# Smaller first part and more seven-product pairs in a feed-forward block, on one core

## The chip, the cores and the metric

The kernel runs on one core of a Trainium2 chip. The metric is device time in microseconds (us) for one launch. Engines are named as in the profile: PE is the matrix engine (TensorE; its weight loads stand apart as PEld), DVE is VectorE, ACT is ScalarE, POOL is GpSimd, SP issues the weight loads. L146 is line 146 of the kernel before.

## The reference, cut to what matters

The kernel computes two layers of an encoder for 256 tokens of width 2048, all in float32: attention in the first, a recurrent block in the second, and behind each a feed-forward block. The change touches the feed-forward block:

```python
x = x + swiglu(rms_norm(x, norm_ffn[i]), ffn_w_gate[i], ffn_w_up[i], ffn_w_down[i])

def swiglu(h, w_gate, w_up, w_down):          # w_gate, w_up: 2048 x 5632, w_down: 5632 x 2048
    return (jax.nn.silu(h @ w_gate) * (h @ w_up)) @ w_down
```

## The kernel before, in words

**Products.** A float32 product is made of three matmuls. A weight tile of 128 x 1024 lands in SBUF (`raw`), ACT rounds it to a high part (`hi`, L145 and L163) and DVE subtracts that to give a low part (`lo`, L146 and L164); activations are split the same way. `product` (L321) then issues high x high, low x high and high x low, each with 512 moving columns.

**Units.** The 5632 hidden features are 44 tiles of 128. A unit is 4 of them; there are 11 units, 0 to 10. `unit` (L754) computes gate and up for its four tiles over the 2048-wide contraction, which is cut into 8 pairs (c = 0 to 7) of two tiles. A pair is done in one of two ways. An *ordinary* pair takes two halves (a gate and an up tile), each 12 matmuls, 24 in all. A *seven-product* pair (`load_seven`, L154) treats the 2 x 2 blocks of weights by Strassen's scheme: 7 products, 21 matmuls. It pays with six more DVE instructions of 512 columns and three more ACT casts: with weight blocks b11, b21 and t1, b22 it needs t1 = b11 + t1 (on DVE at L174 if the three loads ahead were ordinary ones, else by an accumulating DMA that POOL issues at L176), t2 = t1 + b22, t3 = t2 - b11, t4 = b21 + t2 (L169), and a high part (L170) and a low part (L171) of t2, t3 and t4. PE takes them in the order b11, b21, t1, b22, t2, t3, t4. `SEVEN` names the pairs done this way, six of eight; `FEWER` gives shorter lists for the first units.

**End of a unit.** DVE adds up the products (L770 to L773, L791, L794; behind ACT's copy at L769), ACT applies SiLU, DVE multiplies (L795) and transposes 32 x 32 blocks (L408), ACT copies them into place (L416, 16 copies), then ACT and DVE make the high and low part of the hidden tile (L801, L802). With `beside` the copies and the last step are put into `tail` and taken out one piece per `load_seven` of the next unit, 4 copies a piece; without it all 16 stand in one lump.

**Parts.** The down projection is cut along the hidden features into parts (`PARTS`, in tiles). When a part's units are done, its four groups of 512 output columns are computed, two behind each of the next units (`ffn_plan`, L208). Each group is a chunk of 12 matmuls per two hidden tiles. Its two results are scaled by ACT out of PSUM (`form`, L818, two buffers) and added to `x` by an accumulating DMA of POOL (L821). ACT results of every second group are held in `parted` and ordered behind the last cast of the following seven-product pair. The last part goes through `groups` (L355) and DVE.

**What sets the order.** PE's order is the order of the code. A scheduler orders the other engines, within rules: `behind` chains all casts among each other and all DVE work of a split (key "rest") among each other; `ahead` keeps some instructions in front of a coming one. Each engine runs its queue in order. SP loads the weights through 8 `raw` buffers, 7 pairs of `hi`/`lo` hold the parts.

Of the kernel before, what the change touches and what calls it, by code (L numbers as in the profile page):

```python
# [12 lines left out]
F32 = mybir.dt.float32  # L13
# [11 lines left out]
GROUP = NQ // NKV  # L25
NBLK = 8
DFF = 5632
PARTS = [8, 8, 8, 8, 12]
UNIT = 4
SEVEN = (0, 1, 2, 4, 5, 6)  # L30
FEWER = {0: (0, 5, 6), 1: (4, 5, 6), 2: (1, 4, 5, 6)}
HALF = 8
CHUNK = HALF * P
WIDE = 512
# [40 lines left out]
def trunk(ctx, tc, w, out):  # L75
# [17 lines left out]
    def tmp(tag, shape=(P, S), dt=F32, bufs=2):  # L93
        pl = tp if tag in COMMON else scope[-1]
        return pl.tile(list(shape), dt, tag=tag, name=nm(tag), bufs=bufs)
# [9 lines left out]
        )  # L105


    ring, held, ft, ahead, tail, parted = [0], [], [], [], [], []

    def parts(shape):  # L110
        n = ring[0] = (ring[0] + 1) % (RING + MORE)
# [42 lines left out]
    def load_seven(srcs, soon):  # L154
# [20 lines left out]
        else:  # L175
            pool.dma_start(out=t1, in_=b11, accum_op=ALU.add)  # L176
        two(raw[0], ("b11", "b21"))
        two(raw[1], ("t1", "b22"))
        if tail:
            tail.pop(0)()  # L180
        one = [tmp(t, (P, WIDE), F32R) for t in ("ohi", "olo")]
        hi, lo = parts([P, 2, WIDE])
        got["t2"] = tuple(one)
        got["t3"], got["t4"] = ((hi[:, j, :], lo[:, j, :]) for j in range(2))
        t2 = b22
        rests = [
            combine(t2, t1, b22, ALU.add, *got["t2"]),
            combine(b11, t2, b11, ALU.subtract, *got["t3"]),
            combine(b21, t2, b21, ALU.add, *got["t4"]),
        ]  # L190
        while parted:
            follow(parted.pop(), newest["cast"])
        for rest in rests:
            rest()
        return got
# [198 lines left out]
    pool.memset(ones, 1.0)
    idle = ps_m.tile([P, P], F32, tag="pm", name=nm("pm"))
# [354 lines left out]
    def ffn(norm, nxt):  # L750
# [60 lines left out]
        ends = np.cumsum(PARTS) // UNIT  # L811
        for what, i in ffn_plan():
            if what == "unit":
                hid[int(np.searchsorted(ends, i, "right"))] += unit(FEWER.get(i, SEVEN), 0 < i < ends[-1] - 1, (act,) if i < ends[-1] - 1 else (act, dve), i < ends[0])
            else:
                for a, acc in enumerate(wide_project(hid[i[0]], PARTS[i[0]], bank)):
                    t = tmp("form", (P, WIDE))
                    m = act.activation(t, acc, AF.Copy, scale=norm.r[:, a : a + 1])  # L818
# [224 lines left out]
```

## Time and profile before

| | |
|---|---|
| median of 3 runs | 1952.31 us (1952.17 to 1952.49) |
| the profiled execution | 1952.89 us, its span 1951.1 us |
| PE, PEld, DVE, ACT, POOL busy | 99%, 83%, 91%, 74%, 21% of the span |
| matmuls | 9224 |
| granted PE clock | 1.00 |
| first layer's feed-forward | starts near 266 us, ends near 950 us |
| second layer's | starts near 1263 us, ends with the kernel |

A row of the timeline reads: start, busy time, engine, line, operation, output<-inputs, shape, count, and in brackets how long the engine was idle ahead of it and what ended that. A busy time includes the part that overlaps the next instruction on the same engine, so the price of an instruction in a row of them is the distance between starts. A row of the windows has the window's length, then busy time and count for PE, PEld, DVE, ACT and POOL; its count takes in instructions that hang over an edge.

### The profile page before, as it was taken

Reading aid. Unit: us, or ns where it says so; the run is one execution under the profiler, and the core shown is the slowest. Engines: PE = TensorE matmul, PEld = TensorE weight load, DVE = VectorE, ACT = ScalarE, POOL = GpSimd, SP = SyncE. Lnnn points to the kernel's source line nnn. Section 1 sums busy time; section 2 is a strip of 40 time slices with the busy share of each in tenths; the row PEclk is TensorE's granted clock in tenths of the full one; section 3 lists DMA queues with packets and bytes.
Section 4 is the critical chain, followed back from the end, with each engine's and each line's share of the span. In section 5 each row is a group of like instructions: output and inputs, shape, how many; then the busy total and the mean of one; then the engine's idle time right before and its main releaser. Section 6 shows DMA issues by size and latency. Waiting matters only on the chain.

```text
span 1951.1 us, 27630 instructions
## 1 busy us (share of the span) xinstructions
PE 1938.0 (99%) x9224; PEld 1624.0 (83%) x9224; DVE 1768.6 (91%) x2417; ACT 1448.3 (74%) x2358; POOL 401.3 (21%) x497
## 2 busy tenths in 40 slices
PE   9999999999999999999999999999999999999999
PEld 8898888788888888888899998887888888888887
DVE  7878698999999999998799997898999999999993
ACT  7677686777777777777698887866778776787772
POOL 0442250011101111010465450520101111011100
PEclk9999999999999999999999999999999999999999
DMA  8434746698878978787365556555878888788872
GB/s 328 156 127 152 248 158 197 196 272 236 248 233 243 262 240 246 235 244 246 126 223 188 189 164 245 175 194 174 253 236 248 245 248 253 231 246 251 246 257 86
DMA packets 131727, 426.42 MB, mean 219 GB/s; under 512 B 14720, under 2 KB 14976, under 8 KB 131584
## 3 DMA queue, kind: packets, MB, share of 16 engines
q1 hardware_dynamic: 108944, 383.21, 58.0%
q0 software_dynamic: 22496, 41.43, 11.9%
q8 instruction: 72, 1.18, 0.2%
q14 instruction: 71, 0.58, 0.1%
q10 hardware_dynamic: 144, 0.02, 0.0%
HBM read 382.13 MB, written 2.10 MB: 197 GB/s over the span
## 4 chain that ended last, share of the span: by engine, by line
PE 92%; DVE 4%; ACT 1%; issue 1%; DMA 1%; POOL 0%; SPq 0%; ACTq 0%; DVEq 0%; POOLq 0%
PE acc L326 14%; PE acc L323 14%; PE acc L324 14%; PE pm L326 11%; PE pm L323 11%; PE pm L324 11%; PE acc L294 8%; PE acc L292 4%; PE pm L306 1%; PE pm L307 1%; PE pm L305 1%; DVE lo L146 1%; ACT hi L145 1%; DVE lo L164 0%; DMA raw<-in_w_in_dram 0%
## 5 line engine op out<-in xcount | busy, mean ns | idle before, releaser
L146 DVE TENSOR_TENSOR lo<-raw,hi 128x1024 fp32r<-128x1024 f32 (+1 forms) x474 | 574.5, 1240 | 77.1 <-ACT hi L145 75.3
L145 ACT CAST hi<-raw 128x1024 fp32r<-128x1024 f32 (+1 forms) x474 | 478.4, 1045 | 116.5 <-PE acc L324 72.1
L326 PE MATMUL acc<-lo,xg 128*128 128x512 f32 x744 | 290.9, 391 | 2.0 <-DVE lo L146 1.8
L323 PE MATMUL acc<-hi,xg 128*128 128x512 f32 x744 | 290.0, 390 | 0.0
L324 PE MATMUL acc<-hi,xg 128*128 128x512 f32 x744 | 289.6, 389 | 0.0
L164 DVE TENSOR_TENSOR lo<-raw,hi 128x1024 fp32r<-128x1024 f32 x232 | 275.0, 1217 | 6.5 <-ACT hi L163 3.8
L294 PE MATMUL acc<-xg,hi 128*128 128x512 f32 x832 | 271.7, 397 | 0.6 <-ACT hi L145 0.6
L163 ACT CAST hi<-raw 128x1024 fp32r<-128x1024 f32 x232 | 234.6, 1048 | 41.0 <-issue 14.4
L176 POOL DMA_DIRECT2D raw<-raw x90 | 77.7, 863 | 903.9 <-DVE raw L174 369.5
L323 PE MATMUL pm<-hi,act 128*128 128x512 f32 x512 | 199.2, 389 | 0.0
L324 PE MATMUL pm<-hi,act 128*128 128x512 f32 x512 | 199.2, 389 | 0.0
L326 PE MATMUL pm<-lo,act 128*128 128x512 f32 x512 | 199.2, 389 | 0.0
L416 ACT COPY two<-one 32x256 f32<-32x256 f32 x420 | 169.7, 404 | 24.7 <-DVE one L408 16.5
L292 PEld LDWEIGHTS acc<-xg,lo 128*128 128x128 f32 x832 | 156.3, 188 | 35.4 <-DVE lo L146 2.8
L323 PE MATMUL acc<-hi,act 128*128 128x512 f32 x448 | 174.9, 390 | 0.4 <-DVE two L794 0.4
L326 PE MATMUL acc<-lo,act 128*128 128x512 f32 x448 | 174.4, 389 | 0.0
L324 PE MATMUL acc<-hi,act 128*128 128x512 f32 x448 | 174.4, 389 | 0.0
L292 PE MATMUL acc<-xg,lo 128*128 128x256 f32 x832 | 171.8, 281 | 1.2 <-DVE lo L146 1.2
L326 PEld LDWEIGHTS acc<-lo,xg 128*128 128x128 f32 x744 | 139.7, 188 | 34.1 <-DVE lo L146 5.4
L324 PEld LDWEIGHTS acc<-hi,xg 128*128 128x128 f32 x744 | 139.7, 188 | 29.2
L323 PEld LDWEIGHTS acc<-hi,xg 128*128 128x128 f32 x744 | 139.7, 188 | 28.6
L170 ACT CAST hi<-raw 128x512 fp32r<-128x512 f32 x232 | 137.1, 622 | 32.8 <-DVE raw L169 31.8
(221 smaller groups left out, 3852.1 us busy)
## 6 DMA issues: line engine op xcount, KB each, us to landing
raw<-in_w_gate_dram SPq DMA_DIRECT2D x176, 512.0 KB, 4.6
raw<-in_w_up_dram SPq DMA_DIRECT2D x176, 512.0 KB, 5.5
raw<-in_w_down_dram SPq DMA_DIRECT2D x176, 512.0 KB, 4.4
raw<-in_w_in_dram SPq DMA_DIRECT2D x64, 512.0 KB, 4.4
raw<-raw POOLq DMA_DIRECT2D x90, 256.0 KB, 5.8
raw<-in_w_q_dram SPq DMA_DIRECT2D x32, 512.0 KB, 3.8
raw<-in_w_o_dram SPq DMA_DIRECT2D x32, 512.0 KB, 4.2
x<-form POOLq DMA_DIRECT2D x64, 256.0 KB, 6.7
```

Of the source, the lines that this page charges most:

```text
L145: behind("cast", act.copy(hi[:, sl], raw[:, sl]))
L146: behind("rest", dve.tensor_tensor(lo[:, sl], raw[:, sl], hi[:, sl].bitcast(F32), ALU.subtract))
L163: behind("cast", act.copy(hi, src))
L164: behind("rest", dve.tensor_tensor(lo, src, hi[:].bitcast(F32), ALU.subtract))
L170: behind("cast", act.copy(hi, o))
L176: pool.dma_start(out=t1, in_=b11, accum_op=ALU.add)
L292: pe.matmul(acc[:, S:], w, xs[k][:, :S], start=False, stop=stop)
L294: pe.matmul(acc, w, xs[k], start=(k == 0), stop=stop)
L323: pe.matmul(o, xh, wh, start=start, stop=False)
L324: pe.matmul(o, xl, wh, start=False, stop=False)
L326: pe.matmul(o, xh, wl, start=False, stop=stop)
L416: m = (eng.copy if eng is act else eng.tensor_copy)(to[:, :, :, i, :], of[:, :, :, j, :])
```

## The change

The numbers that choose the work change: parts of 4, 8, 8, 8, 8, 8 tiles for 8, 8, 8, 8, 12; units 1 and 2 (the second and the third) get five seven-product pairs for three and four. In `load_seven` the second sum t2 gets a tile of its own (`sum`) and is computed ahead of the low part of t1 and b22; its high part is cast ahead of the piece from `tail`. Unit 0 hands its copies to `tail` too. After a `load_seven` that had evacuations of PSUM ordered behind it (`skip`), the next one takes nothing out of `tail`. To make room, `ones` is set again for the recurrence in place of being kept, and `cs` overwrites its source.

```diff
-PARTS = [8, 8, 8, 8, 12]
+PARTS = [4, 8, 8, 8, 8, 8]
-FEWER = {0: (0, 5, 6), 1: (4, 5, 6), 2: (1, 4, 5, 6)}
+FEWER = {0: (0, 5, 6), 1: (1, 2, 4, 5, 6), 2: (0, 1, 4, 5, 6)}
...
         two(raw[0], ("b11", "b21"))
+        got["t2"] = hi, lo = tuple(tmp(t, (P, WIDE), F32R) for t in ("ohi", "olo"))
+        t2 = tmp("sum", (P, WIDE), bufs=1)
+        behind("rest", dve.tensor_tensor(t2, t1, b22, ALU.add))
         two(raw[1], ("t1", "b22"))
-        if tail:
+        behind("cast", act.copy(hi, t2))
+        if tail and not skip:
             tail.pop(0)()
...
-        t2 = b22
         rests = [
-            combine(t2, t1, b22, ALU.add, *got["t2"]),
+            lambda: behind("rest", dve.tensor_tensor(lo, t2, hi[:].bitcast(F32), ALU.subtract)),
             combine(b11, t2, b11, ALU.subtract, *got["t3"]),
             combine(b21, t2, b21, ALU.add, *got["t4"]),
         ]
         while parted:
-            follow(parted.pop(), newest["cast"])
+            skip.append(parted.pop())
+            follow(skip[-1], newest["cast"])
...
-    ... += unit(FEWER.get(i, SEVEN), 0 < i < ends[-1] - 1, ...)
+    ... += unit(FEWER.get(i, SEVEN), i < ends[-1] - 1, ...)
...
-    cs = cst.tile([P, 32], F32, tag="cs", name="cs")
+    cs = pk[:, PK["lam"] : PK["lam"] + 32]
...
+    ones = tmp("ones", (P, P), bufs=1)
+    pool.memset(ones, 1.0)
     later(SPREAD, nr.spread)
```

The program has 18 matmuls fewer. New work behind units of each layer: two groups of 4 tiles follow unit 1 and unit 2, two of 8 tiles each unit from 3 to 10; before, unit 2 to unit 9 had two of 8 tiles each.

What DVE has in its queue after unit 0 of the first layer, before: the low parts of all four ordinary pairs of unit 1 (`lo` from `raw`, L146; five of them stand just ahead), then the first seven-product pair of unit 1, its fifth pair. `two`/`one` belong to the end of unit 0.

```order
L795 TENSOR_TENSOR two_3221<-two_3221,one_3220 128x1024
L146 TENSOR_TENSOR lo_3696<-raw_3694,hi_3695 128x1024
L146 TENSOR_TENSOR lo_3714<-raw_3712,hi_3713 128x1024
L174 TENSOR_TENSOR raw_3731<-raw_3730,raw_3731 128x512
L164 TENSOR_TENSOR lo_3736<-raw_3730,hi_3735 128x1024
L408 STREAM_TRANSPOSE one_3556<-two_3221 128x1024
L164 TENSOR_TENSOR lo_3740<-raw_3731,hi_3739 128x1024
L169 TENSOR_TENSOR raw_3731<-raw_3731 128x512
L169 TENSOR_TENSOR raw_3730<-raw_3731,raw_3730 128x512 x2
L171 TENSOR_TENSOR olo_3744<-raw_3731,ohi_3743 128x512
L171 TENSOR_TENSOR lo_3746<-raw_3730,hi_3745 128x512 x2
```

The same place now, from the second half of unit 1's first pair on:

```order
L146 TENSOR_TENSOR lo_3590<-raw_3588,hi_3589 128x1024
L174 TENSOR_TENSOR raw_3607<-raw_3606,raw_3607 128x512
L164 TENSOR_TENSOR lo_3612<-raw_3606,hi_3611 128x1024
L798 TENSOR_TENSOR two_3220<-two_3220,one_3219 128x1024
L180 TENSOR_TENSOR sum_3617<-raw_3607 128x512
L164 TENSOR_TENSOR lo_3620<-raw_3607,hi_3619 128x1024
L411 STREAM_TRANSPOSE one_3558<-two_3220 128x1024
L169 TENSOR_TENSOR raw_3606<-sum_3617,raw_3606 128x512 x2
L189 TENSOR_TENSOR olo_3616<-sum_3617,ohi_3615 128x512
L171 TENSOR_TENSOR lo_3629<-raw_3606,hi_3628 128x512 x2
L164 TENSOR_TENSOR lo_3664<-raw_3658,hi_3663 128x1024
```

The seven-product pair now stands behind two halves in place of eight, and another one follows at once. Its second sum (L180) stands ahead of the low part of t1 and b22.

What ACT has in its queue around the start of a unit that follows down groups, before (unit 3): the second cast of pair 0, four copies, the casts of t2, t3 and t4, the two casts of pair 1, four copies, the two evacuations of PSUM (`form` from `pm`) of the second group, then pair 1's t2.

```order
L163 CAST hi_4476<-raw_4468 128x1024
L416 COPY two_3931<-one_4295 32x8x32 x4
L170 CAST ohi_4484<-raw_4468 128x512
L170 CAST hi_4486<-raw_4467 128x512 x2
L163 CAST hi_4523<-raw_4518 128x1024
L163 CAST hi_4527<-raw_4519 128x1024
L416 COPY two_3931<-one_4295 32x8x32 x4
L818 ACTIVATE form_4451<-pm_4377,nr_3161 128x512
L818 ACTIVATE form_4454<-pm_4378,nr_3161 128x512
L170 CAST ohi_4535<-raw_4519 128x512
```

The same place now at the start of unit 2 (that of unit 3 reads alike):

```order
L163 CAST hi_4062<-raw_4050 128x1024
L182 CAST ohi_4058<-sum_4060 128x512
L419 COPY two_3569<-one_3949 32x8x32 x4
L170 CAST hi_4071<-raw_4049 128x512 x2
L821 ACTIVATE form_4033<-pm_3995,nr_3160 128x512
L821 ACTIVATE form_4036<-pm_3996,nr_3160 128x512
L163 CAST hi_4106<-raw_4101 128x1024
L163 CAST hi_4114<-raw_4102 128x1024
L182 CAST ohi_4110<-sum_4112 128x512
L170 CAST hi_4119<-raw_4101 128x512 x2
```

The two evacuations have moved ahead of both casts of pair 1. At the start of units 4 to 9 they stand behind these casts, one on each side of pair 1's t2.

More of the change, by code (lines that the diff above doesn't have):

```diff
@@ L105, in follow @@
         )
-    ring, held, ft, ahead, tail, parted = [0], [], [], [], [], []
+    ring, held, ft, ahead, tail, parted, skip = [0], [], [], [], [], [], []
     def parts(shape):
@@ L177, in load_seven @@
         two(raw[0], ("b11", "b21"))
+        got["t2"] = hi, lo = tuple(tmp(t, (P, WIDE), F32R) for t in ("ohi", "olo"))
+        t2 = tmp("sum", (P, WIDE), bufs=1)
+        behind("rest", dve.tensor_tensor(t2, t1, b22, ALU.add))
         two(raw[1], ("t1", "b22"))
-        if tail:
+        behind("cast", act.copy(hi, t2))
+        if tail and not skip:
             tail.pop(0)()
[L181 to L184, printed above, removed]
-        t2 = b22
+        skip.clear()
+        both = parts([P, 2, WIDE])
+        got["t3"], got["t4"] = (tuple(t[:, j, :] for t in both) for j in range(2))
         rests = [
-            combine(t2, t1, b22, ALU.add, *got["t2"]),
+            lambda: behind("rest", dve.tensor_tensor(lo, t2, hi[:].bitcast(F32), ALU.subtract)),
             combine(b11, t2, b11, ALU.subtract, *got["t3"]),
@@ L391, in trunk @@
     cn = ap.tile([P, 2 * S], F32, tag="cn", name="cn", bufs=1)
-    ones = cst.tile([P, P], F32, tag="ones", name="ones")
+    ones = ap.tile([P, P], F32, tag="ones", name="ones", bufs=1)
     act.dma_start(out=pk[:, :PK0], in_=w["pk"][:, :PK0])
@@ L712, in trunk @@
         attend(h, project(n0.xs), o_t[h])
-    cs = cst.tile([P, 32], F32, tag="cs", name="cs")
+    cs = pk[:, PK["lam"] : PK["lam"] + 32]
     ncs = cst.tile([P, 32], F32, tag="ncs", name="ncs")
     def decay_constants():
-        lam = pk[:, PK["lam"] : PK["lam"] + 32]
+        lam = cs
         e, s, s2, q = (tmp(f"lr{i}", (P, 32), bufs=1) for i in range(4))
@@ L813, in ffn @@
             if what == "unit":
-                hid[int(np.searchsorted(ends, i, "right"))] += unit(FEWER.get(i, SEVEN), 0 < i < ends[-1] - 1, (act,) if i < ends[-1] - 1 else (act, dve), i < ends[0])
+                hid[int(np.searchsorted(ends, i, "right"))] += unit(FEWER.get(i, SEVEN), i < ends[-1] - 1, (act,) if i < ends[-1] - 1 else (act, dve), i < ends[0])
             else:
@@ L821, in ffn @@
                     pool.dma_start(out=x_tm[:, a, i[1] * WIDE : (i[1] + 1) * WIDE], in_=t, accum_op=ALU.add)
+        parted.clear()
         if nxt is not None:
```

## The prediction

> **What bounds the kernel now.** I read the page first, then the windows by stage, then the timelines of DVE, ACT and PE around the first units. The page, first its busy times, then its chain of work:
>
> ```profile
> PE 1938.0 (99%) x9224; PEld 1624.0 (83%) x9224; DVE 1768.6 (91%) x2417; ACT 1448.3 (74%) x2358; POOL 401.3 (21%) x497
> PE 92%; DVE 4%; ACT 1%; issue 1%; DMA 1%; POOL 0%; SPq 0%; ACTq 0%; DVEq 0%; POOLq 0%
> ```
>
> PE sets the end nearly everywhere, so a matmul taken out is worth its distance to the next. The windows give that, and where PE is held up. First layer: unit 1; unit 2 with its eight chunks of down projection; unit 3 with its eight. Last, units 1 and 2 of the second layer:
>
> ```profile
> 307.87:349.75 41.88, 41.88 (x185) 34.19 (x183) 37.38 (x46) 27.32 (x43) 1.73 (x2) 1.00 0.64 210
> 349.75:416.20 66.45, 64.29 (x278) 51.35 (x277) 64.78 (x77) 47.90 (x72) 5.19 (x6) 1.00 0.72 226
> 416.20:477.40 61.20, 61.20 (x272) 50.69 (x271) 60.11 (x75) 45.85 (x67) 7.95 (x10) 1.00 0.83 250
> 1304.90:1413.00 108.10, 105.90 (x460) 85.34 (x459) 101.71 (x121) 74.31 (x113) 6.93 (x8) 1.00 0.69 220
> ```
>
> Unit 3 is six seven-product pairs, two ordinary ones and eight chunks: 6 x 21 + 2 x 24 + 8 x 12 = 270 matmuls (the 272 hang over the edges) in 61.20 us: 0.2267 us each and no wait. A seven-product pair is 21 of them, 4.76 us; an ordinary pair 5.44; a chunk 2.72. Units 1 and 2 are 183 and 276 matmuls, 104.05 us; they take 41.88 + 66.45 = 108.33. So 4.3 us are lost there, in the second layer as much. DVE is busy for 60.11 of 61.20 us in unit 3: it is the next bound, with about a microsecond to spare. Two waits of PE show what the loss is:
>
> ```profile
> 351.20 0.50 PE L326 MATMUL acc<-lo,xg 128*128 128x512 f32 x1 [0.84 <-DVE lo L146]
> 360.42 0.50 PE L323 MATMUL pm<-ohi,fh 128*128 128x512 f32 x1 [1.18 <-ACT ohi L170]
> ```
>
> PE waits for the halves of the weights: DVE and ACT are late.
>
> **What a pair costs DVE.** Its timeline: a seven-product pair of unit 3 and the start of the next one, then five halves of chunks with the end of unit 3 and the start of unit 4:
>
> ```profile
> 435.47 2.36 DVE L164 TENSOR_TENSOR lo<-raw,hi 128x1024 fp32r<-128x1024 f32 x2
> 437.86 0.69 DVE L169 TENSOR_TENSOR raw<-raw 128x512 f32<-128x512 f32 x1
> 438.59 1.29 DVE L169 TENSOR_TENSOR raw<-raw,raw 128x512 f32<-128x512 f32 x2
> 439.80 0.69 DVE L171 TENSOR_TENSOR olo<-raw,ohi 128x512 fp32r<-128x512 f32 x1
> 440.40 1.29 DVE L171 TENSOR_TENSOR lo<-raw,hi 128x512 fp32r<-128x512 f32 x2
> 441.61 2.35 DVE L164 TENSOR_TENSOR lo<-raw,hi 128x1024 fp32r<-128x1024 f32 x2
> ...
> 458.88 5.75 DVE L146 TENSOR_TENSOR lo<-raw,hi 128x1024 fp32r<-128x1024 f32 x5
> 464.56 0.68 DVE L174 TENSOR_TENSOR raw<-raw,raw 128x512 f32<-128x512 f32 x1
> 465.16 1.21 DVE L795 TENSOR_TENSOR two<-two,one 128x1024 f32<-128x1024 f32 x1
> 466.29 1.21 DVE L164 TENSOR_TENSOR lo<-raw,hi 128x1024 fp32r<-128x1024 f32 x1
> 467.43 1.23 DVE L408 STREAM_TRANSPOSE one<-two 128x1024 f32<-128x1024 f32 x1
> 468.59 1.18 DVE L164 TENSOR_TENSOR lo<-raw,hi 128x1024 fp32r<-128x1024 f32 x1
> ```
>
> From start to start a pair takes 441.61 - 435.47 = 6.14 us. A 1024-wide instruction costs 5.68 / 5 = 1.14, a 512-wide one 0.60, but the sum at 437.86 holds its follower, which needs it, for 0.73. With the second sum apart nothing waits for its forerunner: 2 x 1.14 + 6 x 0.60 = 5.87 us. That is the gain of the new tile, 0.27 us per pair of DVE. VectorE: DVE Perf Modes of the Trainium skill (The DRAIN you can't avoid) says that the next instruction starts only when the pipe is empty and that a semaphore between two costs nothing more; by it the pair would stay at 6.14. The rows differ, 0.60 against 0.73, and I go by them.
>
> So each pair turned into a seven-product one gives PE 0.68 us and costs DVE 5.87 - 2 x 1.14 = 3.6.
>
> **The change, part by part.** *18 matmuls fewer:* 18 x 0.2267 = 4.1 us, 2.04 per layer; all of it on the path only where PE isn't waiting.
>
> *Units 3 to 10 at full lists:* no term. PE has no wait there in unit 3, and DVE gets 6 x 0.27 = 1.6 us of slack per unit. The second sum now needs t1 ahead of the cast that used to need it first. Its one buffer costs nothing: the last reader, DVE's low part of t2, stands ahead of the next sum in DVE's own queue. POOL's DMA for it lands in time: issued at 432.30 it takes 5.8 us, to 438.1, for a sum that would be due at 441.61 + 1.14 = 442.75.
>
> ```profile
> 432.30 0.86 POOL L176 DMA_DIRECT2D raw<-raw  x1 [5.93 <-DMA raw<-in_w_up_dram]
> raw<-raw POOLq DMA_DIRECT2D x90, 256.0 KB, 5.8
> x<-form POOLq DMA_DIRECT2D x64, 256.0 KB, 6.7
> ```
>
> *Eight more evacuations per layer* (the additional part): ACT 0.66 each of 45.85 / 61.20 busy, POOL an accumulating DMA each; hidden by PE except where they stand ahead of a cast (below). Bounds: 0 and the latter.
>
> *The last unit:* PE waits 0.4 us for it now, since only the 8 chunks that are ready cover it; now 8 chunks of another part and 4 ready ones do, so -0.4 per layer. The norm behind the first layer gets four groups in a shorter time; 0 to +2 us, I take 0.
>
> ```profile
> 885.09 0.50 PE L323 MATMUL acc<-hi,act 128*128 128x512 f32 x1 [0.21 <-DVE two L794]
> ```
>
> *`ones` and `cs`:* a memset of 0.20 us on POOL (its row at the kernel's start), and nothing: 0, up to the same 0.2.
>
> ```profile
> 0.73 0.20 POOL L394 MEMSET ones<- 128x128 f32 x1 [0.29 <-POOLq L1034]
> ```
>
> *Units 1 to 3* decide. Unit 0's end now, on DVE, then the copies on ACT that are one lump:
>
> ```profile
> 302.20 0.69 DVE L770 TENSOR_TENSOR one<-one,pm 128x512 f32<-128x512 f32 x1 [0.81 <-ACT one L769]
> 308.68 5.76 DVE L146 TENSOR_TENSOR lo<-raw,hi 128x1024 fp32r<-128x1024 f32 x5
> 328.08 0.69 DVE L171 TENSOR_TENSOR olo<-raw,ohi 128x512 fp32r<-128x512 f32 x1 [4.19 <-ACT ohi L170]
> ...
> 320.76 6.64 ACT L416 COPY two<-one 32x256 f32<-32x256 f32 x16 [1.11 <-DVE one L408]
> ```
>
> At 302.20 DVE waits for PE's products, so it enters unit 1 with no lead, and this holds after the change. The lump goes: -4.2 us for DVE. But in unit 1 two seven-product pairs now follow one ordinary pair. From 308.68 DVE owes, by the order: one half 1.14, t1 0.60, five pairs 29.35, unit 0's product, transposition and low part 3.44, pair 3's and the first half of pair 7's lows 3.42: 346.6. ACT adds waits, since t3's and t4's casts stand behind copies that need the transposition: +0.4 in pair 1, about 1 more in pairs 2, 3 and 5. So 348.0. PE, unhindered, is at pair 7 at 307.87 + 2 x 5.44 + 5 x 4.76 = 342.55 and wants that low part two matmuls on, at 343.0. Unit 1 loses 5.0 us (3.6 without ACT's waits) and ends at 353.0.
>
> Behind it stand only 4 chunks, 10.9 us of PE, in which DVE must do the unit's end and the next pair 0. By the same sums DVE ends pair 0 of unit 2 at 368.1, in time (PE: 364.0 to 368.7). ACT's prices, from unit 3 and the start of unit 4:
>
> ```profile
> 412.09 1.99 ACT L163 CAST hi<-raw 128x1024 fp32r<-128x1024 f32 x2
> 414.11 1.65 ACT L416 COPY two<-one 32x256 f32<-32x256 f32 x4
> 415.78 1.35 ACT L818 ACTIVATE form<-pm,nr 128x512 f32<-128x512 f32 x2
> 417.03 0.61 ACT L170 CAST ohi<-raw 128x512 fp32r<-128x512 f32 x1
> ```
>
> ACT casts t4 till 367.5, then come both evacuations (1.25), which now stand ahead of pair 1's casts (0.95): its high part is there at 369.7, 0.95 late, its low part at 370.85. From there the pair ends at DVE's pace, 2.5 us late; pair 2 adds 0.25. Unit 2 loses 2.75; its pairs 2 and 3, ordinary, then let DVE catch up.
>
> Unit 3 has the full list behind 4 chunks. Here too the evacuations stand ahead of pair 1's casts: its high part is there 0.3 us after PE reaches that pair, and DVE starts on it then. From there DVE owes, to the first half of pair 7: five pairs 29.35, three halves 3.42, the low part of unit 2's tile 1.14 and 0.3 of waiting, 34.2. PE needs 29.2 for pairs 1 to 6 and 0.45 for the two matmuls it does first: 0.3 + 34.2 - 29.2 - 0.45, unit 3 loses 4.9. Unit 4 has eight chunks ahead of it again and recovers.
>
> Sum per layer: 5.0 + 2.75 + 4.9 = 12.65 for the 4.3 lost today, -2.04 for the matmuls, -0.4 at the end: +5.9. Two layers: +11.8. Against the profiled execution's own 1952.89 (span 1951.1 and 1.8 around it) that is 1964.7; the median of the runs is 0.6 lower, 1952.31: **1964.1**.
>
> Bounds of the loss: DVE alone, never held up by ACT. From 302.20 to the first half of pair 7 of unit 3 it owes 16 pairs (93.9), 23 halves (26.1), 4 sums t1 (2.4), three unit ends (25.6): 148.0, at 450.2. PE unhindered wants it at 307.87 + 2 x (40.12 + 10.88) + 34.0 + 0.45 = 444.3. So at least 5.9 per layer is lost. Above: the evacuations of unit 3 also wait for one of the two `form` buffers, that is for POOL's 6.7 us DMA behind a DMA for pair 2: up to +1.1 per layer, and the norm's +2: 1964.1 + 2.2 + 2 = 1968.3.
>
> **The rivals.** A measurement of this kernel can tell about 0.2%, 3.9 us, from no change: faster is below 1948.4, slower above 1956.2.
>
> *A. DVE alone.* ACT's waits are covered and the loss is the 5.9: 5.9 - 4.3 - 2.04 - 0.4 = -0.8 per layer, 1950.6, no change. For it: DVE has next to no idle time in unit 3; against: the 4.19 us above.
>
> *B. Faster.* The lows that PE wants come in time because ACT's lump, the reason for a lateness of 4.2 us in unit 1, is gone, and DVE's lead over PE at unit 1 is larger than the 0 that I read. It decides from a loss under 4.7 per layer; at today's 4.3 it gives -2.4 per layer, 1947.4. Against: the 302.20 row, where DVE waits for PE's own products.
>
> *C. The new tile saves nothing:* 16 pairs x 0.27 = 4.3 per layer more, 1972.7. Against it stand the rows at 437.86 and 439.80. The page of the Trainium skill named above speaks for it.
>
> *D. POOL's accumulating DMAs are too late* for the second sums of units 3 to 10, where eight more DMAs per layer share the queue. Above the spare 4.6 us every microsecond costs one per unit, 8 units and two layers: 1980 for one.
>
> **How the numbers follow.** Forecast 0.55, A 0.20, B 0.13, C 0.06, D 0.06. The range reaches from B, 1947.0, to the forecast's upper bound, 1969.0; C and D stay out, 0.12. Faster is B, 0.13; no change is A and a little of the forecast's low end, 0.22; slower the rest, 0.65.
>
> **What would show it.** Right: in both layers units 1 to 3 with their 16 chunks, 720 matmuls or 163.2 us, take 173 to 178 us on PE, with waits for `lo` and `hi` in pairs 1 and 6; evacuations right ahead of pair 1's casts in units 2 and 3, with DVE idle behind them; later units without waits; DVE's pair at 5.9 us. Wrong: a loss of under 5 us in these units, or waits of PE in units 4 to 9.

## The result, and the profile after

The changed kernel takes 1986.4 us (median of 4 runs, 1985.1 to 1987.8), the kernel before 1952.2 beside it: a ratio of 1.0175, 95% interval 1.0157 to 1.0192. The forecast was 1964.1, with 1969.0 as its upper end: the sign and most of the places are right, the size is a third of what came. The page after, its busy times and its chain:

```profile
PE 1954.1 (98%) x9206; PEld 1618.1 (82%) x9206; DVE 1781.4 (90%) x2453; ACT 1463.8 (74%) x2392; POOL 424.3 (21%) x520
PE 78%; DVE 9%; ACT 5%; issue 4%; DMA 3%; POOL 1%; SPq 0%; ACTq 0%; DVEq 0%; POOLq 0%
```

The 18 matmuls are gone, but PE has fallen from 92% of the chain to 78%. The windows show where; the borders are the starts of units 0 to 4 in the first layer, then of units 1 to 4 in the second (a unit with the chunks behind it):

```profile
266.51:310.14 43.63, 42.05 (x184) 34.27 (x183) 40.17 (x60) 32.57 (x56) 14.33 (x21) 1.00 0.55 174
310.14:367.37 57.23, 54.58 (x227) 41.30 (x225) 55.40 (x68) 38.27 (x57) 5.14 (x6) 1.00 0.70 206
367.37:421.17 53.80, 52.69 (x226) 41.77 (x225) 50.95 (x64) 39.88 (x59) 6.98 (x8) 1.00 0.78 231
421.17:491.10 69.93, 65.54 (x271) 49.49 (x270) 64.84 (x82) 51.34 (x76) 7.88 (x10) 1.00 0.80 232
1323.69:1382.63 58.94, 55.06 (x226) 41.15 (x226) 57.34 (x71) 39.34 (x59) 5.14 (x6) 1.00 0.68 201
1382.63:1436.93 54.30, 53.02 (x226) 41.69 (x225) 51.08 (x64) 39.76 (x59) 5.97 (x8) 1.00 0.74 224
1436.93:1507.28 70.35, 66.19 (x272) 50.64 (x270) 64.83 (x82) 51.49 (x76) 8.98 (x12) 0.98 0.81 232
```

Unit 0 has 183 matmuls, units 1 and 2 with their 4 chunks 225 each, unit 3 with its 8 has 270. At 0.2267 us each that is 41.5, 51.0, 51.0 and 61.2. What the window is longer by, I call its loss: 2.2, 6.2, 2.8 and 8.7 us in the first layer, 7.9, 3.3 and 9.1 in the second, where unit 0 loses nothing. Units 1 to 3 take 181 and 183.6 us, not 173 to 178.

One more piece lies between the two feed-forward blocks: the norm and the recurrence, which the change touches only by `ones` and `cs`. Its window before and after:

```profile
949.86:1263.38 313.52, 312.42 (x1797) 274.30 (x1796) 278.66 (x443) 264.59 (x460) 144.87 (x186) 1.00 0.58 193
```

```profile
963.41:1282.21 318.80, 314.81 (x1797) 275.34 (x1796) 279.41 (x441) 267.44 (x468) 150.63 (x195) 0.99 0.57 189
```

It has the same 1797 matmuls and takes 5.3 us more. The granted clock of 0.99 in that window doesn't explain it: the kernel "unit 3 five", below, has 1.00 in this stretch and takes 318.7 us for it. Against before, the first layer's feed-forward is 13.4 us longer (696.90 against 683.47), the stretch between 5.3, the rest from the second layer on 14.5 (to the spans' ends): 33.2 of the 33.3 us by which the spans differ.

The longest wait of PE in each feed-forward block of the kernel after stands in unit 3's first pair. PE there, in the first layer:

```profile
425.70 0.50 PE L326 MATMUL pm<-ohi,fh 128*128 128x512 f32 x1 [1.64 <-ACT form L821]
427.78 0.50 PE L326 MATMUL pm<-hi,fh 128*128 128x512 f32 x1 [1.12 <-ACT form L821]
```

PE doesn't wait for weights but for its output: the banks that the down groups left are still to be read by ACT. Unit 2's first pair has the same wait, shorter:

```profile
371.13 0.50 PE L326 MATMUL pm<-ohi,fh 128*128 128x512 f32 x1 [0.88 <-ACT form L821]
```

ACT in unit 3's first pair (the evacuations of the first part's third group, then of its fourth), then POOL:

```profile
414.57 0.69 ACT L821 ACTIVATE form<-pm,nr 128x512 f32<-128x512 f32 x1 [1.00 <-PE pm L329]
...
424.96 0.69 ACT L821 ACTIVATE form<-pm,nr 128x512 f32<-128x512 f32 x1 [0.66 <-DMA x<-form]
427.04 0.69 ACT L821 ACTIVATE form<-pm,nr 128x512 f32<-128x512 f32 x1 [1.40 <-DMA x<-form]
```

```profile
418.07 0.86 POOL L176 DMA_DIRECT2D raw<-raw  x1 [5.43 <-DMA raw<-in_w_up_dram]
418.61 2.10 POOL L824 DMA_DIRECT2D x<-form  x2
425.94 0.86 POOL L824 DMA_DIRECT2D x<-form  x1 [5.23 <-ACT form L821]
```

Read it backwards: the fourth group needs a `form` buffer, both are held until POOL's DMAs land, and those two, the first of which had its data at 415.26, are issued at 418.61, behind a DMA for t1 that waited 5.43 us for its load. Then DVE, from the same unit's second pair to its fourth (an ordinary one), and ACT in the third:

```profile
428.70 1.23 DVE L164 TENSOR_TENSOR lo<-raw,hi 128x1024 fp32r<-128x1024 f32 x1 [3.59 <-ACT hi L163]
...
434.59 1.23 DVE L164 TENSOR_TENSOR lo<-raw,hi 128x1024 fp32r<-128x1024 f32 x1
435.72 0.69 DVE L180 TENSOR_TENSOR sum<-raw 128x512 f32<-128x512 f32 x1
436.32 1.23 DVE L164 TENSOR_TENSOR lo<-raw,hi 128x1024 fp32r<-128x1024 f32 x1
...
440.97 2.36 DVE L146 TENSOR_TENSOR lo<-raw,hi 128x1024 fp32r<-128x1024 f32 x2 [0.18 <-ACT hi L145]
```

```profile
436.52 0.62 ACT L182 CAST ohi<-sum 128x512 fp32r<-128x512 f32 x1 [1.10 <-DVE sum L180]
437.17 1.66 ACT L419 COPY two<-one 32x256 f32<-32x256 f32 x4
438.85 1.14 ACT L170 CAST hi<-raw 128x512 fp32r<-128x512 f32 x2
```

The first of the two pairs takes DVE 434.59 - 428.70 = 5.89 us, as forecast. The second, which carries four copies from `tail`, takes 440.97 - 434.59 = 6.38: ACT waits for the sum with the copies behind the cast, and then the casts of t3 and t4 come late for DVE.

### The profile page after: what moved, and what is told of

Same layout as the page of the kernel before. It is cut to its first block, busy times and chain, and to the rows that moved or that the text cites. A ratio compares the mean times of both kernels' runs of the same rounds, so it can differ in the third digit from the quotient of the medians.

```text
span 1984.4 us, 27704 instructions
## 1 busy us (share of the span) xinstructions
PE 1954.1 (98%) x9206; PEld 1618.1 (82%) x9206; DVE 1781.4 (90%) x2453; ACT 1463.8 (74%) x2392; POOL 424.3 (21%) x520
## 3 DMA queue, kind: packets, MB, share of 16 engines
q8 instruction: 72, 1.18, 0.2%
## 4 chain that ended last, share of the span: by engine, by line
PE 78%; DVE 9%; ACT 5%; issue 4%; DMA 3%; POOL 1%; SPq 0%; ACTq 0%; DVEq 0%; POOLq 0%
PE acc L329 11%; PE acc L326 11%; PE acc L327 11%; PE pm L329 10%; PE pm L327 10%; PE pm L326 10%; PE acc L297 8%; PE acc L295 4%; DVE lo L146 2%; ACT two L419 1%; DVE lo L164 1%; DMA x<-form 1%; ACT hi L145 1%; PE pm L309 1%; PE pm L310 1%
## 5 line engine op out<-in xcount | busy, mean ns | idle before, releaser
L146 DVE TENSOR_TENSOR lo<-raw,hi 128x1024 fp32r<-128x1024 f32 (+1 forms) x462 | 563.6, 1246 | 76.6 <-ACT hi L145 75.7
L164 DVE TENSOR_TENSOR lo<-raw,hi 128x1024 fp32r<-128x1024 f32 x244 | 297.7, 1220 | 19.2 <-ACT hi L163 18.9
L329 PE MATMUL acc<-lo,xg 128*128 128x512 f32 x708 | 278.6, 393 | 4.0 <-DVE lo L146 2.4
L326 PE MATMUL acc<-hi,xg 128*128 128x512 f32 x708 | 276.5, 391 | 0.0
L327 PE MATMUL acc<-hi,xg 128*128 128x512 f32 x708 | 276.0, 390 | 0.0
L163 ACT CAST hi<-raw 128x1024 fp32r<-128x1024 f32 x244 | 247.1, 1048 | 38.2 <-PE pm L327 16.2
L327 PE MATMUL pm<-hi,act 128*128 128x512 f32 x576 | 224.1, 389 | 0.0
L326 PE MATMUL pm<-hi,act 128*128 128x512 f32 x576 | 224.1, 389 | 0.0
L329 PE MATMUL pm<-lo,act 128*128 128x512 f32 x576 | 224.1, 389 | 0.0
L171 DVE TENSOR_TENSOR lo<-raw,hi 128x512 fp32r<-128x512 f32 x244 | 160.2, 691 | 23.6 <-ACT hi L170 18.6
L182 ACT CAST ohi<-sum 128x512 fp32r<-128x512 f32 x122 | 75.7, 621 | 111.8 <-DVE sum L180 110.6
L169 DVE TENSOR_TENSOR raw<-sum,raw 128x512 f32<-128x512 f32 x244 | 156.4, 681 | 0.0
L327 PEld LDWEIGHTS acc<-hi,xg 128*128 128x128 f32 x708 | 133.1, 188 | 28.0
L326 PEld LDWEIGHTS acc<-hi,xg 128*128 128x128 f32 x708 | 133.1, 188 | 26.2
```

The lines of the kernel that those rows point to most:

```text
L146: behind("rest", dve.tensor_tensor(lo[:, sl], raw[:, sl], hi[:, sl].bitcast(F32), ALU.subtract))
L163: behind("cast", act.copy(hi, src))
L164: behind("rest", dve.tensor_tensor(lo, src, hi[:].bitcast(F32), ALU.subtract))
L169: behind("rest", dve.tensor_tensor(o, x, y, op))
L171: return lambda: behind("rest", dve.tensor_tensor(lo, o, hi.bitcast(F32), ALU.subtract))
L326: pe.matmul(o, xh, wh, start=start, stop=False)
```

## The experiments

My theory after the result: four waits on in-order queues (unit 0, the copies, unit 3's buffers, the norm) beside the debt of DVE that I had forecast. The rival: DVE's debt is simply larger than forecast. The table has what every run lost by place, in us, first and second layer, worked out as above for each unit ("rest" is the units from 4 on and the last part, losses under 0.15 as 0), and the stretch between the blocks. These places are read from one profiled execution of each kernel, the ratios from all its runs; each ratio is against the kernel before as measured beside it (1952.2 for the kernel after, 1952.8 to 1953.4 for the others).

| kernel | ratio (95%) | unit 0 | unit 1 | unit 2 | unit 3 | rest | between |
|---|---|---|---|---|---|---|---|
| before | 1 | 0, 0 | 0.4, 0.4 | 3.9, 3.9 | 0, 0 | 0.5, 0.5 | 313.5 |
| after | 1.0175 (1.0157-1.0192) | 2.2, 0 | 6.2, 7.9 | 2.8, 3.3 | 8.7, 9.1 | 0, 0.9 | 318.8 |
| tile alone | 1.0025 (1.0015-1.0035) | 2.4, 0 | 0, 0 | 4.1, 3.8 | 0, 0 | 2.4, 0.9 | 315.3 |
| old parts | 1.0129 (1.0114-1.0144) | 2.2, 0 | 6.2, 8.0 | 9.4, 9.5 | 0, 0 | 1.0, 2.8 | 312.7 |
| old lists | 1.0078 (1.0061-1.0095) | 2.2, 0 | 0, 0 | 0, 0 | 8.1, 8.3 | 0.2, 0 | 318.9 |
| POOL's order | 1.0148 (1.0133-1.0163) | 2.2, 0 | 6.2, 8.0 | 2.9, 2.8 | 6.5, 6.5 | 0, 0.8 | 319.0 |
| last part 16 | 1.0277 (1.0262-1.0292) | 2.5, 0 | 6.3, 8.1 | 2.8, 3.0 | 8.9, 9.0 | 14.4, 13.5 | 312.2 |
| piece first | 1.0147 (1.0132-1.0162) | 2.3, 0 | 5.4, 7.2 | 3.1, 3.1 | 5.9, 6.8 | 0, 0 | 320.6 |
| unit 3 five | 1.0122 (1.0105-1.0139) | 2.5, 1.3 | 6.2, 6.2 | 2.8, 2.8 | 4.9, 4.6 | 0, 0.8 | 318.7 |
| tile, piece first | 1.0012 (1.0002-1.0021) | 0.2, 0 | 1.9, 0 | 5.1, 4.0 | 0, 0 | 0.5, 0.5 | 313.8 |
| second layer four | 0.9983 (0.9975-0.9992) | 0, 0 | 0.4, 0.4 | 4.0, 0 | 0, 0 | 0.5, 0 | 313.7 |
| second layer five | 0.9991 (0.9982-1.0000) | 0, 0 | 0.4, 0.4 | 4.2, 0 | 0, 2.5 | 0.5, 0 | 314.3 |
| both layers four | 0.9993 (0.9984-1.0002) | 0, 0 | 0.4, 0.4 | 0, 0 | 0, 0 | 0, 0 | 318.6 |
| all repairs | 1.0103 (1.0090-1.0117) | 0, 0 | 7.2, 6.8 | 3.1, 3.3 | 3.0, 3.3 | 0, 0 | 320.0 |
| copies ahead | 0.9999 (0.9989-1.0008) | 0, 0 | 0.4, 0.4 | 0, 0 | 0, 0 | 0, 0 | 319.2 |
| row ahead of add | 0.9991 (0.9982-1.0000) | 0, 0 | 0.4, 0.4 | 0, 0.2 | 0, 0 | 0, 0 | 317.5 |

**The parts of the change.** The tile alone, then the kernel after with the old parts, then with the old lists:

```diff
+PARTS = [8, 8, 8, 8, 12]                                # tile alone, old parts
+FEWER = {0: (0, 5, 6), 1: (4, 5, 6), 2: (1, 4, 5, 6)}   # tile alone, old lists
+        if tail:                                        # tile alone, old lists
+    ... += unit(FEWER.get(i, SEVEN), 0 < i < ends[-1] - 1, ...)   # tile alone, old lists
```

> The kernel before with the edits for the second sum's own tile alone (`sum` ahead of the low part of t1 and b22, its cast ahead of the piece from `tail`, room made in `ones` and `cs`); parts and lists as before, unit 0 without `tail`, no `skip`. My theory: DVE gets 0.27 us per seven-product pair, seven pairs in units 1 and 2, which lose 4.3 us per layer today; at most 1.9 per layer comes back: 1949.5 (1948.0 to 1951.5), a seven-product pair of DVE in unit 5 at 5.87 us against 6.14. Rival, the tile saves nothing: 1952.2 and 6.14.

> The kernel after with the parts of before (8, 8, 8, 8, 12); five pairs in units 1 and 2, the own tile, unit 0 through `tail` and `skip` stay. My theory: the lists cost about 8 us of DVE's lateness per layer in units 1 and 2 (in place of 4.3), less 2.04 for the matmuls, while unit 3's first pair and the norm behind the first layer cost nothing: 1952 to 1959, no loss at the start of unit 3, 313.5 us between the two feed-forward blocks. Rival, the lists and not the parts make the loss: 1975 or more.

> The kernel after with the lists of before (three pairs in unit 1, four in unit 2), unit 0 without `tail` and no `skip`; parts of 4, 8, 8, 8, 8, 8 and the own tile stay. My theory: two thirds of the loss come with the parts: about 8 us per layer in unit 3, whose first pair waits for banks of PSUM, about 2 in units 1 and 2 together, 5 behind the first layer, so 1964 to 1974. Rival, the parts are harmless and the lists make the loss: 1950 to 1955.

Measured: 1957.6, 1978.0 and 1967.7. With 1986.4 for the whole that makes a table of two by two on the tile's kernel: the lists alone add 20.4, the parts alone 10.1, both 28.8. ("Lists" takes in unit 0's copies through `tail` and the rule on `skip`, which change with them here.) So neither is harmless, and the tile, which was to pay for them, is 4.6 us slower than the kernel before. My expectation held for the old lists only: with nothing but the parts changed against the tile alone, unit 3 loses 8 us more and the stretch between is 3.6 us longer. For the tile alone it fell, rival included: a pair of DVE in unit 5 takes 5.89 us (from 561.09 to 566.98) as expected, but the kernel is slower than both. And for the old parts the rival's number came: with no chunks between unit 1 and unit 2, unit 2's first pair loses 8.2 us. ACT, then PE there:

```profile
363.98 1.65 ACT L419 COPY two<-one 32x256 f32<-32x256 f32 x4 [4.61 <-DVE one L411]
365.65 1.14 ACT L170 CAST hi<-raw 128x512 fp32r<-128x512 f32 x2
```

```profile
366.33 0.79 PE L326 MATMUL pm<-hi,fh 128*128 128x512 f32 x1 [2.97 <-ACT hi L170]
```

The copies of unit 1's result wait 4.61 us for its transposition, and the casts of t3 and t4 of unit 2's first pair stand behind them. The new parts put four chunks there, which hide it: parts and lists belong together, but not for the reason that I had costed.

Where does the tile lose? The spans of the two executions differ by 5.4 us: 2.4 come in unit 0 of the first layer, 1.6 in its units 8 and 9, 1.8 in the stretch between, less some small gains. ACT and PE of the tile's kernel in unit 0:

```profile
293.43 0.63 ACT L182 CAST ohi<-sum 128x512 fp32r<-128x512 f32 x1 [0.85 <-DVE sum L180]
293.95 0.91 ACT L469 ACTIVATE form<-two,pk 128x256 f32<-128x256 f32 x2
...
299.36 0.62 ACT L477 CAST fh<-form 128x512 fp32r<-128x512 f32 x1 [1.42 <-POOL form L475]
```

```profile
300.03 0.50 PE L326 MATMUL pm<-hi,fh 128*128 128x512 f32 x1 [1.13 <-ACT fh L477]
```

The scheduler now has the cast of t2, which waits for the sum, ahead of forming the last block of activations, and PE waits for that block. In the kernel before that forming stood ahead of the same cast.

**POOL's order.** Two DMAs change places with one, that of unit 3's third pair; no other engine's order changes.

```diff
-            pool.dma_start(out=t1, in_=b11, accum_op=ALU.add)
+            late = pool.dma_start(out=t1, in_=b11, accum_op=ALU.add)
...
+                for d in added[1:]:
+                    follow(late, d)
...
-                    pool.dma_start(out=x_tm[:, a, ...], in_=t, accum_op=ALU.add)
+                    d = pool.dma_start(out=x_tm[:, a, ...], in_=t, accum_op=ALU.add)
+                    if i == (0, 2):
+                        added.append(d)
```

> The kernel after with one edit on POOL: in each layer the two accumulating DMAs of the third group of the first part (x from form) are issued ahead of the DMA for t1 of unit 3's third pair, not behind it; nothing moves on any other engine. My theory: unit 3's first pair waits for banks of PSUM because ACT waits for the two form buffers, which POOL's DMA frees late behind one that waits for its load; it is freed 2 to 3 us earlier, the waits of 3.3 and 4.9 us there go for the most part, and a half of what is won comes back as DVE's lateness in pairs 1 to 6: 1978 to 1983. Rival, DVE's debt sets unit 3's end: waits only move to lo and hi in pair 1 and later, 1985 to 1987.

Measured 1981.9, unit 3 at 6.5 in both layers. POOL, ACT and PE:

```profile
415.47 0.86 POOL L830 DMA_DIRECT2D x<-form  x1 [2.60 <-ACT form L827]
```

```profile
424.10 1.26 ACT L827 ACTIVATE form<-pm,nr 128x512 f32<-128x512 f32 x2
```

```profile
424.83 0.50 PE L332 MATMUL pm<-ohi,fh 128*128 128x512 f32 x1 [0.87 <-ACT form L827]
```

The DMA leaves 3.1 us earlier, ACT no longer waits for a buffer, PE's wait for the bank is 0.87 and the second one is gone. It is shown: the buffer chain makes 2.2 and 2.6 us of unit 3. The other 6.5 stay.

**The copies' place, a shorter list, a longer last part.** Piece first puts ACT's copies ahead of the cast of t2 again; unit 3 five builds on POOL's order; the third changes the parts.

```diff
-        behind("cast", act.copy(hi, t2))     # piece first: below the two lines that follow
         if tail and not skip:
             tail.pop(0)()
+        behind("cast", act.copy(hi, t2))
...
+FEWER = {..., 3: (1, 2, 4, 5, 6)}            # unit 3 five
+PARTS = [4, 8, 8, 8, 16]                     # last part 16
```

> The kernel after with one edit: in load_seven the piece from `tail` (ACT's four copies) stands ahead of the cast of t2 again, as it did before the change, not behind it. My theory: with the cast first, ACT waits 1.1 us for the sum in every pair, then does cast, copies and the casts of t3 and t4 in a row, and the pair takes 6.39 us on DVE where it carries a piece against 5.9 without; with the copies in that wait every pair takes 5.9 on DVE, units 1 and 3 lose about 1.5 us less each: 1977 to 1983. Rival, DVE's own work sets the pace of these pairs whatever ACT does: 1985 to 1988 and 6.3 to 6.4 us as before this edit.

> The kernel with POOL's order edited (1981.9) and a list of five for unit 3 too (pairs 1, 2, 4, 5, 6; its first pair an ordinary one). My theory: what is left of unit 3's loss there, 6.5 us, is DVE's and ACT's debt; an ordinary first pair saves DVE 3.6 us and costs PE three matmuls, 0.68: unit 3 loses 2 to 3.5 us and the time is 1974 to 1978. Rival, the evacuations of the first part's last group make the loss wherever they stand: unit 3 loses 5.5 or more, 1980 to 1983.

> The kernel after with parts of 4, 8, 8, 8, 16: the last part has 16 tiles, so that the four groups of the last part, between which the norm behind the first layer works, are 8 chunks (21.8 us) apart for three of them in place of 4 (10.9 us). My theory: the 5.3 us lost behind the first layer (318.8 us between the two feed-forward blocks against 313.5) come from norm work that queues up in these short groups: 313 to 314.5 us between, 1981 in all (1979.5 to 1982.5), units 0 to 3 as in the kernel after. Rival, the re-made `ones` or `cs` and the new order make it: 318 to 319 us between, 1985 to 1988.

Measured: 1981.6, 1977.3 and 2007.6. Piece first: DVE and ACT in the same pair as shown above for the kernel after:

```profile
432.31 1.23 DVE L164 TENSOR_TENSOR lo<-raw,hi 128x1024 fp32r<-128x1024 f32 x1
...
438.19 2.37 DVE L146 TENSOR_TENSOR lo<-raw,hi 128x1024 fp32r<-128x1024 f32 x2
```

```profile
433.18 1.66 ACT L420 COPY two<-one 32x256 f32<-32x256 f32 x4
434.86 0.62 ACT L184 CAST ohi<-sum 128x512 fp32r<-128x512 f32 x1
435.91 1.22 ACT L170 CAST hi<-raw 128x512 fp32r<-128x512 f32 x2 [0.44 <-DVE raw L169]
```

With the copies in the time in which ACT would wait for the sum, the pair takes 5.88 and DVE has no gap. So the place of ACT's copies, not DVE's own work, made these pairs 6.38. For the kernel the edit is worth 4.8 us, which isn't the pairs alone: PE's waits for banks in unit 3's first pair get shorter too (by 1.4 and 0.8 us of loss), and the stretch between gets 1.8 longer. In the units, too, it isn't all gain: in unit 1's second pair the copies then wait for the transposition with the cast behind them (4.3 us in the second layer). Unit 3 five: an ordinary first pair takes unit 3 from 6.5 to 4.9 and 4.6, less than I expected, but the time falls inside what I gave.

Last part 16: the stretch between is 312.2, as the theory wanted, and `ones` and `cs` are as in the kernel after. So it is the parts that make the 5.3. The whole is 21 us slower than the kernel after all the same, outside what I and the rival gave, since no chunks stand between units 9 and 10 now; unit 10 loses 12.05 us in each layer, by the same wait as above:

```profile
844.23 1.65 ACT L419 COPY two<-one 32x256 f32<-32x256 f32 x4 [5.23 <-DVE one L411]
```

I hadn't seen that coming, though the run with the old parts showed it at unit 2.

**The tile with ACT's two places mended.**

```diff
+        if tail:
+            tail.pop(0)()
+        newest["ohi"] = act.copy(hi, t2)
+        behind("cast", newest["ohi"])
...
+                if soon and c == seven[-1] - 1 and not hid[0]:
+                    follow(newest["ohi"], newest["forming", seven[-1]])
```

> The kernel with the second sum's tile alone (1957.6, parts and lists of before) with two edits of ACT's order: the piece from `tail` ahead of the cast of t2, and in the first unit of the first layer the forming of the last block of activations ahead of the cast of t2 of the pair before it. My theory: the tile alone was 4.6 us slower than the kernel before because of these two places: unit 0's wait of 2.2 us goes, the waits at the ends of units 8 and 9 (1.4 us) go, unit 2 loses 2 to 3.5 in place of 4.1 and 3.8: 1948.5 to 1952. Rival, the tile has a cost of its own on DVE or POOL: 1955 to 1958.

Measured 1955.3. The waits of unit 0 and of the units 8 and 9 are gone, as the theory said, but the time is the rival's: still 2.5 us slower than before. Unit 2 loses 5.1 and 4.0, no less than without the tile. So 0.27 us per pair of DVE buys nothing here: unit 2's loss isn't made of DVE's debt alone. PE's longest wait there, 1.76 us, is for the cast of t2, which stands on ACT behind the copies, and these wait 3.98 us for the transposition (1.18 and 3.37 us in the kernel before). Whether the tile has a cost of its own besides, no run shows. A wait of 0.94 us for a low part in unit 1 is new; why, stays open.

**A version that beats both.** If four chunks hide a unit's end and short lists keep DVE out of debt, the new parts should serve the kernel before, without the new tile. In the second layer no norm follows. The third kernel has the second layer's numbers in both. (The lists are shortened here.)

```diff
-PARTS = [8, 8, 8, 8, 12]
+PARTS_OF = [[8, 8, 8, 8, 12], [4, 8, 8, 8, 8, 8]]
+FEWER_OF = [FEWER, {**FEWER, 3: (1, 4, 5, 6)}]    # five: 3: (1, 2, 4, 5, 6)
...
+        parted.clear()
```

> The kernel before (no tile of its own for t2) with parts of 4, 8, 8, 8, 8, 8 in the second layer alone, where no norm follows, and there a list of four for unit 3 too (pairs 1, 4, 5, 6), as unit 2 has it. My theory: four chunks ahead of unit 2 and of unit 3 with short lists cover both units, so the 3.9 us that unit 2 loses in that layer go; six matmuls more cost 1.4: 1949 to 1951. Rival, the eight more evacuations delay unit 3 whatever its list: 1952 or more.

> As the kernel above with a list of five for unit 3 of the second layer (pairs 1, 2, 4, 5, 6). My theory: three matmuls fewer than with four, 0.7 us, but a loss of 2 to 3 in unit 3 for DVE's debt: 1950 to 1953, slower than with four by 1 to 2. Rival, unit 3 has DVE time left with an ordinary first pair: 1948.5 to 1950.

> As the kernel with four for unit 3, but in both layers. My theory: the first layer wins the same 2 to 3 us in units 2 and 3 and loses 5 behind it, since the norm meets groups of 4 chunks, with `ones` kept as before: 318 to 319.5 us between the two feed-forward blocks, 1951 to 1954.5. Rival, the 5.3 us behind the first layer come of the re-made `ones` or the new tile: 313.5 between, 1946.5 to 1949.

Measured: 1950.1, 1951.8 and 1952.4, all inside what the theory gave. Units 1 to 3 of the second layer with a list of four:

```profile
1304.52:1471.57 167.05, 167.05 (x737) 137.83 (x735) 154.38 (x183) 119.10 (x177) 15.62 (x18) 1.00 0.77 235
```

735 matmuls are 166.6 us; 0.4 are lost, where the kernel before loses 4.3 in units 1 and 2, and DVE isn't busy for 12.7 us. The fifth pair in unit 3 saves 0.7 and costs 2.5. With the new parts in the first layer too, its units lose as little, but the stretch between goes to 318.6, with `ones` kept and no new tile: once more the parts. The first of the three is the fastest kernel of the study, 0.17% ahead of the kernel before (interval 0.08 to 0.25).

**All repairs.** POOL's order, the list of five for unit 3, the copies' place and the forming's place, all in the kernel after (edits as above).

> The kernel after with all four repairs together: POOL's order at unit 3, a list of five for unit 3, the piece from `tail` ahead of the cast of t2, and the forming of the last activation block ahead of the cast of t2. My theory: what is left is DVE's debt in units 1 to 3 (about 5, 2.8 and 3 us per layer) and the norm: 1968 to 1974. Rival, the repairs pay for the same waits and don't add up: 1975 to 1978.

Measured 1973.7, inside the theory's range: 12.7 of the 34 us are order, buffers and unit 3's shorter list. What stays is 13.4 us of loss per layer in units 1 to 3, and the norm. Unit 1 isn't at the 5 that I gave but at 7: some 4.2 us of it fall in its second pair, where the copies now wait 4.07 us for the transposition with the cast of t2 behind them. In the kernel after, with the cast ahead, that pair loses 1.7 and 2.3: the copies' new place costs here a part of what it saves elsewhere.

**The norm.** The kernel with lists of four in both layers, with one row of ACT moved (copies ahead), then with a row of DVE moved as well (row ahead of add).

```diff
+                follow(m, newest["moved"])         # the last group's squares behind the copies before
...
+                    follow(m, newest["turned", 8]) # the last group's add behind the second group's xg
```

> The kernel with parts of 4, 8, 8, 8, 8, 8 and lists of 3, 3, 4, 4 in both layers (1952.4) with one edit of ACT's order in the norm behind the first layer: the eight copies of the third group's blocks stand ahead of the squares of the last group, not between its two. My theory: a large part of the 5.3 us lost there is not norm work that doesn't fit in but one row out of place: ACT waits for PE's last group with the copies behind it, and DVE's transposition of the last group waits for them; the transposition comes some 3 us earlier, 314.5 to 316 us lie between the two feed-forward blocks in place of 318.6: 1948.5 to 1950.5. Rival, the work of two groups doesn't fit into the time of one whatever its order: 318 to 319 between, 1951.5 to 1953.

> The kernel of the run before with one more edit, on DVE: the fourth low part of the second group's activations (xg) stands ahead of the residual add of the last group, not behind it. My theory after the last run: the copies of the third group's blocks, on ACT and POOL, wait for that row, since it is the last reader of their one buffer `two`, and it stands on DVE behind an add that waits 2.7 us for PE's last group. With it ahead the copies start 3 us earlier; the squares of the last group, which can't be earlier than its add, then set DVE's reduction and transposition: some 1.8 us earlier, 316 to 317.5 us between the two feed-forward blocks in place of 318.6 to 319.2: 1950 to 1951.5. Rival, the amount of norm work behind the last group sets the time and not a row: 318 to 319.5 between, 1952 to 1953.

Measured 1952.6 and 1951.2. The first theory fell: the copies stood ahead and started some 0.3 us earlier, not 3. ACT and DVE in that run show why:

```profile
946.71 3.31 ACT L417 COPY two<-one 32x256 f32<-32x256 f32 x8 [1.71 <-DVE xg L439]
```

```profile
945.53 0.75 DVE L350 SCALAR_TENSOR_TENSOR x<-acc,nr,x 128x512 f32<-128x512 f32 x1 [2.74 <-PE acc L327]
946.20 0.47 DVE L439 SCALAR_TENSOR_TENSOR xg<-two,pk,xg 128x256 fp32r<-128x256 f32 x1
...
952.74 1.24 DVE L409 STREAM_TRANSPOSE one<-x 128x1024 f32<-128x1024 f32 x1
```

The copies overwrite `two`, whose last reader is one `xg` of the group before, and that row stands on DVE behind an add that waits 2.74 us for PE. With it ahead, DVE again:

```profile
941.51 1.63 DVE L441 SCALAR_TENSOR_TENSOR xg<-two,pk,xg 128x256 fp32r<-128x256 f32 x4
945.48 0.75 DVE L350 SCALAR_TENSOR_TENSOR x<-acc,nr,x 128x512 f32<-128x512 f32 x1 [2.34 <-PE acc L327]
...
950.88 1.24 DVE L411 STREAM_TRANSPOSE one<-x 128x1024 f32<-128x1024 f32 x1
```

The last transposition comes 1.9 us earlier, the stretch between is 1.1 to 1.7 shorter and the time 1.2 to 1.4. Both are what was expected; the intervals of the three kernels overlap, so the rows carry this and not the medians. The other 3.9 us of this stretch's loss stay open: more such rows, or work that doesn't fit between groups of 4 chunks. The trace says where they lie. PE waits here, as the kernel before doesn't:

```profile
957.81 0.50 PE L295 MATMUL acc<-xg,hi 128*128 128x512 f32 x1 [2.12 <-DVE xg L441]
```

And its granted clock is 0.50 from 960.25 to 963.66, by which PE loses up to 1.7 us (half of 3.41, an estimate). The second isn't needed for a long stretch: "unit 3 five" has 318.7 with a clock of 1.00, and other waits in its place.

## Why the prediction was right and wrong, step by step

- **18 matmuls, -4.1:** right; the count is 9206, and the layers' sums close with it. **The last unit, -0.4:** right; the kernel before loses 0.5 there, the kernel after nothing. **Units 4 to 10 without waits:** right in the first layer; 0.9 is lost in unit 4 of the second.
- **DVE's pair at 5.87:** the size was right (5.89 at 428.70), the use was not. In the pairs that carry copies it is 6.38, more than the 6.14 of before. The step that failed is "that is the gain of the new tile": the same edit moved ACT's copies behind the cast of t2, and I priced no such move. VectorE: DVE Perf Modes of the Trainium skill (The DRAIN you can't avoid) was weighed there as a reason why the tile might save nothing; the rows at 435.72 and 436.32, 0.60 apart, with the first busy for 0.69, don't bear it out: the second starts before the first ends. The same section says that a next instruction that isn't held starts earlier, so it spoke for rival C less than I took it to. C's premise fell with these rows. The tile alone made the kernel slower all the same, by ACT's order as far as the runs show a cause.
- **Unit 0 and the lump:** "The lump goes: -4.2 us for DVE" counted a gain in unit 1 and no cost in unit 0. Unit 0 loses 2.2 in the first layer, through a row of ACT that the scheduler moved, with the tile alone as well; put back, it is 0 to 0.2.
- **Unit 1, 5.0:** 6.2 and 7.9. Mechanism right (waits for `olo` and `lo` in pairs 1, 2, 3, 5 and 6; with three pairs in the list the loss is 0). Too small, in part for the 6.38, since piece first takes 0.7 to 0.8 off in each layer; in the second layer 1.2 of it falls in the first pair, behind a low part that PE waits 0.88 us for; why, stays open. **Unit 2, 2.75:** 2.8 and 3.3, but the agreement is partly luck. 1.2 us fall in pair 0, which I had in time, by the wait for a bank at 371.13; pair 1 loses 1.1 where I had 2.5, pair 2 0.3 as forecast.
- **Unit 3, 4.9, up to 1.1 more for the buffers:** 8.7 and 9.1. This is the largest failed step. The chain by `form` and POOL's queue was named, but as a delay of DVE only, and at 1.1: I hadn't read that PE's own banks of the next unit hang on the same evacuations. Moving POOL's two DMAs gives 2.2 and 2.6 back. Of the 6.5 that stay against 4.9, 1.2 fall in pair 0 with PE's wait for a bank (0.87); the rest falls in pairs 1 to 7 behind low parts, which fits DVE's debt with the copies' wait in it.
- **The norm, 0 to +2, taken as 0:** 5.3, outside my own bound. This step failed too. I saw that four groups come in a shorter time and didn't ask which rows of the norm stand between them. Parts with a last part of 12 or 16 have 312.2 to 315.3 between, those with 8 have 317.5 to 320.6, whatever else changes.
- **`ones` and `cs`, 0:** no cost that a run shows. PE waits 0.69 us for the new `ones`, where the kernel before waits 0.73 for `dg`, and the kernel with 16 tiles re-makes it too and has 312.2.
- **The rivals:** A and B needed a loss of at most 5.9 per layer in units 1 to 3; it was 17.7 and 20.3. D fell: but for unit 4 of the second layer no unit from 4 on loses more than 0.15.

From the forecast's +11.8 to 33.3: unit 0 2.2, unit 1 1.2 and 2.9, unit 2 0 and 0.6, unit 3 3.8 and 4.2, unit 4 0.9, the norm 5.3; 21.1 in all, to within 0.4.

## What to carry to other kernels

When an edit shortens the cover of a place (here 12 tiles to 8, 8 to 4), list what stands on every in-order queue there, and price the row that waits together with everything behind it: five of the waits here were ready work behind a row that waited for something else. PSUM banks and small buffers tie queues together, so a late DMA on POOL can stop PE by way of ACT (2.2 and 2.6 us here). Put short work into the wait of an engine (the copies ahead of the cast), but not where that work has a wait of its own.

## What the runs showed of the hardware that I had not expected

PE after its longest wait in the second layer of the kernel after:

```profile
1442.65 0.50 PE L326 MATMUL pm<-ohi,fh 128*128 128x512 f32 x1 [2.83 <-ACT form L821]
1442.98 0.57 PE L327 MATMUL pm<-ohi,fl 128*128 128x512 f32 x1
...
1444.95 0.63 PE L329 MATMUL pm<-lo,fh 128*128 128x512 f32 x1
1445.38 0.63 PE L326 MATMUL acc<-hi,xg 128*128 128x512 f32 x1
...
1446.57 0.39 PE L326 MATMUL pm<-hi,xg 128*128 128x512 f32 x1
1446.80 0.40 PE L327 MATMUL pm<-hi,xg 128*128 128x512 f32 x1
```

The first matmul behind a wait is followed after 0.33 us, not 0.227, so such a wait costs 0.1 more than its row says. And from the third on they stand further apart, 0.43 in most rows, until 1446.57: nine matmuls take 3.92 us in place of 2.04. The granted clock is 0.50 from 1443.04 to 1446.45, and 0.98 over unit 3's window. So behind this wait PE was 1.9 us slower, but the unit lost little by it: PE then waits less for low parts in pair 1, which loses 0.1 us in place of 1.25 in the first layer, where the clock stays at 1.00, and the losses of unit 3 are 9.1 and 8.7. TensorE: Matmul & The Clock Gate of the Trainium skill (Part 1: The HAM clock gate) says that the clock halves behind an idle window of about 3.4 us; the rate, 0.43 for 0.227, and the granted 0.50 agree with a halved clock, but here a wait of 2.83 us was enough, and in the kernel with the old parts one of 2.97 behind three shorter ones. Shorter waits can do it, and needn't: in the kernel after the clock is at 0.50 from 972.0 to 975.4, with a wait of 1.66 us ending at 970.81, while in "unit 3 five" waits of 1.55 and 2.11 us at 967.41 and 972.68 left it at 1.00. What decides, no run here shows.
